# SwiGLUs: where the modulation chunks stand, and ScalarE's copies of running sums ahead of the late parts of a gate product

## The chip, the cores and the metric

One core of a Trainium2 chip runs one inference step. The metric is the device time of the program in microseconds; the median of three runs before the change is 2295.45 (2293.73 to 2296.03).

The core's engines work side by side, each through its own list of instructions in order, and wait for each other by semaphores: TensorE (PE, with its weight loads PEld), VectorE (DVE), ScalarE (ACT), GpSimd (POOL) and the queue that issues most loads (SP).

## The reference

Two layers of a hybrid diffusion model, on 128 prompt and 512 sample tokens of width 1024. Each layer has a SwiGLU, a mixer (convolution with a gMLP unit in the first layer, windowed attention in the second) and another SwiGLU, each with a modulated norm ahead of it and a gated residual behind:

```python
def swiglu(h, wg, wu, wd):
    return (jax.nn.silu(h @ wg) * (h @ wu)) @ wd

def modulation(cond, w_mod, b_mod):
    m = jax.nn.silu(cond) @ w_mod + b_mod
    return m.reshape(cond.shape[0], N_MOD, D_MODEL)
...
for l in range(DEPTH):
    mp = modulation(c_ctx[None, :], w_mod[l], b_mod[l])
    ms = modulation(c, w_mod[l], b_mod[l])
    xs = residual(xs, swiglu(pre(xs, ms, norm_w[l, 0], 0), *f1), ms, norm_w[l, 1], 0, 0.5)
    ...
    xs = residual(xs, swiglu(pre(xs, ms, norm_w[l, 4], 2), *f2), ms, norm_w[l, 5], 2, 0.5)
```

The inner width is 2816. All inputs are float32.

## The kernel before

**Numbers.** A float32 operand is split into a high part (ScalarE copies it, rounded) and a low part (VectorE subtracts the high part from the original). `mm3` multiplies with three matmuls: high by high, high by low, low by high. So each weight tile needs a load into one of three `raw` buffers (512 KB), a ScalarE copy and a VectorE subtraction before TensorE can use it, and the raw buffer is free again after the subtraction.

**A SwiGLU** (`ffn`) runs over 22 blocks `j` of 128 inner columns, cut into four parts: blocks 0 to 5, 5 to 10, 10 to 16 and 16 to 22 in the first SwiGLU (`PARTS`), 0 to 4, 4 to 10, 10 to 16 and 16 to 22 in the other three (`PARTS7`). Each part makes its gate products, then, but for the last part, a down-projection (`down`) multiplies them by their rows of `wd` and adds the result to `ys` in memory by GpSimd's DMA: ten products (two halves by five token tiles), each copied out of PSUM by ScalarE. The `between` list has what is issued after each of the ten; the `mods` list how many modulation chunks.

**Plain blocks.** The blocks of the first two parts of the first SwiGLU, and of the first part of the others, are computed as they stand (`unit`): for a group of 384 and one of 256 tokens, the gate and the up product of a block, then `glu`. `weights(j)` loads and splits a block's `wg` and `wu`. In the second part `sums_between(2)` puts one step of the running block sums (`block_sums`, 24 steps, mostly on VectorE) ahead of every second of a unit's eight `k` steps.

**Transformed blocks** (`group`). The later parts use a seven-product scheme on half-size operands. Per block `j` there are seven products `p1` to `p7` of 12 matmuls each; `p1`, `p6`, `p5` and `p3` accumulate one after another in the same PSUM tile `A[j]`, and the running sum is copied out between them (`e1`, `e6`, `e5`, ScalarE, into the tiles `sp` and `up`), before the next product may overwrite it. `p2` goes to another tile and `p7`, `p4` to a third, which VectorE adds or subtracts (`e2`, `e7`, `e4`). `e3` is the silu. `e4` ends with the product `s` of silu and up, a 128x640 tile, and its split into high and low: the gate product `gs[j]` that the down-projection reads. TensorE's order (`steps`) in the block of `j` is p1(j), p3(j-1), p6(j), p4(j-1), p7(j), p5(j), p2(j); p1, p2, p6, p7, p5 for a part's first block. `go` issues a product, then what copies out the products before it (`settle`), then the fill work of that step.

**Fill work.** `prep(j)` makes the weights of a block: g0 and g1 split the gate's raw tile (for p1 and p2), s2 forms sums of raw tiles on VectorE, t0 and t1 split those (p3, p6), s0 and s1 split another sum, `rawx`, which GpSimd's DMA accumulates (p7, p5), u0 and u1 split the rest (p4). The even ones run on ScalarE, the odd ones and s2 on VectorE. `fills(j+1)` spreads the next block's over the seven steps; the weights of a part's first block are made in the `between` list of the down-projection ahead of it.

**Modulation chunks.** The modulation of the coming sub-layers is computed on VectorE in the background: `background(n)` takes n chunks from a list; each (`mod_chunk`) loads 512 KB of `wmodT` into a raw buffer and reduces it twice against `cbc`, which `setup_cbc` loads and ScalarE runs through silu. 54 chunks are spread over the first SwiGLU, 33 each over the second and third, 8 over the fourth; `drain` does what is left at the end. `background_ahead` starts the load of the next chunk.

The order on TensorE, VectorE and ScalarE is that in which the code issues the instructions (`InOrder`, line 71, which is the line of all of them in the profile). SP's order is made by a scheduler, but it issues in order too: a load that waits for a raw buffer holds up those behind it.

Of the kernel before, what the change touches and what calls it, by code (L numbers as in the profile page):

```python
# [17 lines left out]
NT = 5  # L18
# [14 lines left out]
GA, GB = (0, 384), (384, 640)  # L33
GROUPS = [GA, GB]

PARTS7 = [(0, 4), (4, 10), (10, 16), (16, 22)]
HT = T // 2

# [51 lines left out]
class Builder:  # L90
# [550 lines left out]
    def ffn(self, l, i, h, lead, nxt, fetches, started=None):  # L641
# [4 lines left out]
        gs, ws = started or ({}, {})  # L646
        slot = 2 * i
        bounds = PARTS if started else PARTS7
        since = bounds[2][0] if started else bounds[1][0]

        def weights(j):
            if j not in ws:
                ws[j] = [self.take(*self.ffn_weight(l, i, j, w)) for w in ("wg", "wu")]
            return ws[j]

        def unit(j, g, inserts=None):
            if j not in gs:
                gs[j] = self.pair()
            self.glu(*self.proj2(weights(j), h, g, inserts), gs[j], g)
# [43 lines left out]
        def parts(pr):  # L703
            return [tuple(u[:, n * 512:n * 512 + 512] for u in pr) for n in range(pr[0].shape[-1] // 512)]
# [17 lines left out]
        def prep(j):  # L722


            def s2():
                r = raws["t", j] = raws["g", j]
                V.tensor_tensor(out=r[:, 512:1024], in0=raws["s", j][:, 512:1024], in1=r[:, 512:1024], op=ALU.add)
                V.tensor_tensor(out=r[:, 0:512], in0=r[:, 512:1024], in1=r[:, 0:512], op=ALU.add)

            g = halves("g", j, (2, j), (1, j))  # L730
            s = halves("s", j, (7, j), (5, j))
            t = halves("t", j, (3, j), (6, j))
            u = halves("u", j, (4, j), (4, j + 1)) if j in pairs else [lambda: None] * 2
            return dict(g0=g[0], g1=g[1], s2=s2, t0=t[0], t1=t[1], s0=s[0], s1=s[1], u0=u[0], u1=u[1])
# [61 lines left out]
        def e4(j):  # L796
            V.tensor_tensor(out=up[j][:, fh], in0=E.pop(j), in1=up[j][:, fh], op=ALU.subtract)
            s, u = sp.pop(j), up.pop(j)
            V.tensor_tensor(out=s, in0=s, in1=u, op=ALU.mult)
            gs[j] = self.pair()  # L800
            self.split(s, *gs[j])

        def run(fs):
            for f in fs:
                f()
# [13 lines left out]
        def sums_between(every=1):  # L819
            return {k: lambda: run([tops.pop(0) for _ in range(1) if tops]) for k in range(0, KC, every)}  # L820

        evacs = {p1: e1, p2: e2, p3: e3, p4: e4, p5: e5, p6: e6, p7: e7}
        late, done = [], set()

        def settle():

            for f, j in late[:]:
                if f is not p7 or (p5, j) in done:
                    late.remove((f, j))
                    evacs[f](j)  # L830
                    done.add((f, j))

        def go(f, j, *then):
            f(j)
            settle()
            late.append((f, j))
            run(then)

        def fills(n):

            if n >= NJ:
                return [[] for _ in range(7)]
            w = prep(n)
            return [[], [w["g0"]], [w["g1"]], [lambda: load_up(n), w["s2"]] if n in pairs else [w["s2"]], [w["t0"]],
                    [w["t1"], lambda: load_gate(n + 1) if n + 1 < ends[n] else None],
                    [w["s0"], w["s1"], lambda: load_sums(n + 2) if n + 2 < NJ else None]]

        def steps(j0, j1):

            r = [(p1, j0), (p2, j0), (p6, j0), (p7, j0), (p5, j0)]  # L850
            for j in range(j0 + 1, j1):
                r += [(p1, j), (p3, j - 1), (p6, j), (p4, j - 1), (p7, j), (p5, j), (p2, j)]
            return r

        def group(j0, j1, wd):


            fs = []
            ahead, mod = [self.background_ahead], [lambda: self.background(1)]
            for j in range(j0, j1):  # L860
                w = prep(j)
                f = fills(j + 1) if j + 1 < j1 else [[], [], wd[0:1], [], wd[1:2], [], wd[2:3]]
                u = [w["u0"], w["u1"]] if j in pairs else []
                if j == j0:
                    f = [u + ahead + f[1], f[2] + f[3], mod + f[4], f[5], ahead + f[6]]
                else:
                    f[0] = u + f[0]
                    if j + 1 < j1:
                        f[1] = f[1] + mod
                    if j + 2 < j1:  # L870
                        f[5] = f[5] + ahead
                fs += f
            for (p, j), f in zip(steps(j0, j1), fs):
                go(p, j, *f)
            go(p3, j1 - 1, *wd[3:4])
            go(p4, j1 - 1, *wd[4:])
            settle()

        ys = {(t, half): self.dram([P, 512], "ys") for t in range(NT) for half in range(2)}

        def down(j0, j1, pi, wd):

            gp = [gs.pop(j) for j in range(j0, j1)]
            loads, wd2 = wpieces(1, j0, j1)
            if j1 < since:
                between = [loads, [], [], [], [], [], [lambda: weights(j1)], [], [], []]
                mods = [0, 2, 2, 1, 1, 1, 0, 1, 1, 1]
            else:
                n = prep(j1)
                between = [loads, [], [], [lambda: load_gate(j1)], [],  # L890
                           [n["g0"], n["g1"]], [n["s2"], n["t0"]], [n["t1"], lambda: load_gate(j1 + 1)],
                           [lambda: load_up(j1), n["s0"]], [n["s1"], lambda: load_sums(j1 + 2)]]
                mods = [0, 2, 2, 1, 1, 0, 0, 0, 0, 0]
            n = j1 - j0 - 1
            for half in range(2):
                for t in range(NT):
                    if half or t > 1:
                        ps = self.ps()
                        self.proj_tok(ps, gp, (wd, wd2)[half], t)
                    elif t == 0:  # L900

                        two = self.ps(), self.ps()
                        for ks in (range(n), [n]):
                            for u in range(2):
                                self.proj_tok(two[u], gp, wd, u, ks)
                        ps = two[0]
                    else:
                        ps = two[1]
                    o = self.tmp(512)
                    copy(o, ps)  # L910
                    nc.gpsimd.dma_start(out=ys[t, half], in_=o, **(dict(accum_op=ALU.add) if pi else {}))  # L911
                    run(between.pop(0))
                    self.background(mods.pop(0))

        for pi, (j0, j1) in enumerate(bounds[:-1]):
            loads, wd = wpieces(0, j0, j1)
            if j0 >= since:
                group(j0, j1, loads)
            elif not started:
                load_sums(since)  # L920
                load_sums(since + 1)
                unit(1, GB, sums_between())
                weights(3)
                unit(2, GB, sums_between())
                todo = sums_between()
                todo[2] = lambda then=todo[2]: (then(), run(loads))
                unit(3, GA, todo)
                run(tops)
                unit(3, GB)
            else:  # L930
                if j0 == 0:
                    unit(1, GB)
                    self.setup_cbc()
                    unit(2, GA)
                    weights(3)
                    self.background(2)
                    unit(2, GB)
                    self.background(2)
                else:
                    load_sums(since)  # L940
                    load_sums(since + 1)
                for j in range(max(j0, 3), j1):
                    weights(j)
                    if j + 1 < j1:
                        weights(j + 1)
                    else:
                        run(loads)
                    for n, g in enumerate(GROUPS):
                        unit(j, g, sums_between(2) if j0 else None)
                        self.background(1 if j0 else 2)  # L950
                if j0:
                    run(tops)
            down(j0, j1, pi, wd)
        j0, j1 = bounds[-1]
        rows = self.gate_rows(l, slot, True)
# [1011 lines left out]
```

## Time and profile before

| | us |
|---|---|
| median of three runs | 2295.45 |
| profiled execution | 2296.32 |
| its span, first to last instruction | 2294.6 |
| TensorE busy | 2244.4 |
| VectorE busy | 1635.3 |
| ScalarE busy | 1042.9 |

The profile is of one execution. A row of the timeline begins with the time from the span's start and the length of the stretch, then engine, operation, what is written from what, the shape and how many instructions are merged in it; a bracket is the engine's idle time just before, and what ended it. A wait for several things is put down to the one that came last. Modulation chunks show as `scr<-raw,cbc`, weight splits as `w<-raw`, running-sum copies as ACT `tmp<-ps 128x320`, gate products' splits as `act<-tmp 128x640`. Matmuls `ps<-sum,w` occur only in transformed parts; their first ones start at 269 us in the first SwiGLU, at 802, 1249 and 1941 in the others.

### The profile page before, as it was taken

To read this page: it belongs to the slowest core of one execution; us is meant where nothing else is said; L and a number is where in the kernel's file an instruction comes from. 1 tells how busy PE (TensorE), PEld (TensorE's weight loads), DVE (VectorE), ACT (ScalarE), POOL (GpSimd) and SP (SyncE) were. 2 spreads that over 40 slices of the span, in tenths; PEclk is the share of its full clock that TensorE was granted. 3 is DMA by queue.
4 is the path that set the end of the run, shared out by engine and by line. 5 is a ranking of instruction groups with operands and counts; after the bars stand their busy time and mean duration, and the time that the engine had idled before them with its cause. 6 is when DMAs were issued, how large, how long until landed. Compare 5 with 4: busy or idle time off the path is not lost.

```text
span 2294.6 us, 35306 instructions
## 1 busy us (share of the span) xinstructions
PE 2244.4 (98%) x13692; PEld 2037.1 (89%) x13692; DVE 1635.3 (71%) x2738; ACT 1042.9 (45%) x1841; POOL 263.7 (11%) x364
## 2 busy tenths in 40 slices
PE   9989999999999999999999999999999999999998
PEld 7979898989889898989897989898976797989897
DVE  5688686876966885868778868687588578636366
ACT  5223343453246443434454434345568563434342
POOL 1000101011002011110021111101110021111100
PEclk9999999999999999999999999999999999999999
DMA  8574877553224477777546777765310345665645
GB/s 298 175 234 150 215 188 194 156 187 99 87 92 120 162 205 184 206 177 198 210 129 191 193 192 198 191 177 195 101 32 10 136 123 185 174 136 154 139 126 181
DMA packets 143049, 372.71 MB, mean 162 GB/s; under 512 B 15233, under 2 KB 21761, under 8 KB 142113
## 3 DMA queue, kind: packets, MB, share of 16 engines
q1 hardware_dynamic: 109328, 302.55, 38.9%
q0 software_dynamic: 33552, 67.90, 16.9%
q8 instruction: 107, 1.75, 0.3%
q14 instruction: 62, 0.50, 0.1%
HBM read 322.90 MB, written 42.25 MB: 159 GB/s over the span
## 4 chain that ended last, share of the span: by engine, by line
PE 69%; DVE 13%; DMA 7%; issue 5%; ACT 4%; POOL 1%; DVEq 0%; SPq 0%; ACTq 0%; POOLq 0%
PE ps L71 69%; DMA raw<-wmodT 4%; DVE scr L71 3%; DVE tmp L71 3%; DVE w L71 3%; DMA rawx<-ws 2%; ACT w L71 2%; ACT tmp L71 1%; DVE raw L71 1%; ACT act L71 1%; POOL nwq L71 1%; DVE Y L71 1%; DMA ys<-tmp 1%; DVE act L71 0%; ACT sum L71 0%
## 5 line engine op out<-in xcount | busy, mean ns | idle before, releaser
L71 PE MATMUL ps<-act,w 128*128 128x320 f32 (+6 forms) x6024 | 915.5, 319 | 21.3 <-DVE w L71 8.9
L71 PEld LDWEIGHTS ps<-act,w 128*128 128x128 f32 (+1 forms) x6024 | 847.5, 185 | 53.3 <-issue 18.3
L71 PE MATMUL ps<-w,act 128*128 128x512 f32 (+1 forms) x3480 | 781.6, 384 | 1.4 <-ACT act L71 1.3
L71 PEld LDWEIGHTS ps<-w,act 128*128 128x128 f32 x3480 | 624.3, 188 | 136.8 <-ACT act L71 2.6
L71 DVE TENSOR_TENSOR w<-raw,w 128x1024 fp32r<-128x1024 f32 (+1 forms) x340 | 409.1, 1216 | 205.1 <-ACT w L71 198.0
L71 PE MATMUL ps<-sum,w 128*128 128x320 f32 x3168 | 485.4, 311 | 13.8 <-ACT tmp L71 13.8
L71 PEld LDWEIGHTS ps<-sum,w 128*128 128x128 f32 x3168 | 473.6, 190 | 17.1 <-ACT tmp L71 17.0
L71 ACT ACTIVATE w<-raw 128x1024 fp32r<-128x1024 f32 (+1 forms) x340 | 350.6, 1047 | 205.6 <-DVE raw L71 107.3
L71 DVE CUSTOM_DVE_ANT_0 scr<-raw,cbc 128x1024 bf16<-128x1024 f32 x256 | 313.3, 1224 | 92.8 <-DMA raw<-wmodT 87.0
L71 ACT ACTIVATE tmp<-ps 128x320 f32<-128x320 f32 (+4 forms) x450 | 209.1, 469 | 371.8 <-PE ps L71 317.4
L71 ACT ACTIVATE act<-tmp 128x256 fp32r<-128x256 f32 (+4 forms) x238 | 114.9, 497 | 363.6 <-DVE tmp L71 363.5
L71 DVE TENSOR_TENSOR act<-tmp,act 128x256 fp32r<-128x256 f32 (+4 forms) x240 | 124.2, 525 | 117.0 <-ACT act L71 115.8
L911 POOL DMA_DIRECT2D ys<-tmp x120 | 90.9, 774 | 661.8 <-ACT tmp L71 653.5
L689 POOL DMA_DIRECT2D rawx<-ws x66 | 79.6, 1208 | 653.4 <-DMA rawx<-ws 189.3
L71 DVE TENSOR_TENSOR w<-rawx,w 128x1024 fp32r<-128x1024 f32 x66 | 80.8, 1224 | 27.3 <-ACT w L71 25.7
L71 DVE TENSOR_TENSOR tmp<-ps,tmp 128x320 f32<-128x320 f32 x132 | 64.0, 485 | 22.4 <-PE ps L71 21.3
L71 DVE TENSOR_TENSOR tmp<-tmp,tmp 128x640 f32<-128x640 f32 (+1 forms) x98 | 68.8, 715 | 6.4
L71 ACT ACTIVATE tmp<-ps,sh,G 128x256 f32<-128x256 f32 (+1 forms) x120 | 60.3, 525 | 22.8 <-PE ps L71 22.7
L71 ACT ACTIVATE w<-rawx 128x1024 fp32r<-128x1024 f32 x66 | 69.4, 1052 | 0.0
L71 DVE TENSOR_TENSOR tmp<-tmp,ps 128x320 f32<-128x320 f32 (+2 forms) x110 | 52.7, 479 | 18.0 <-ACT tmp L71 17.2
L71 ACT ACTIVATE tmp<-Y 128x1024 bf16<-128x1024 f32 (+1 forms) x35 | 32.6, 932 | 57.5 <-DVE Y L71 57.5
L71 ACT ACTIVATE Y<-X 128x1024 f32<-128x1024 f32 x30 | 31.7, 1058 | 54.6 <-DVE X L71 50.6
(162 smaller groups left out, 1242.0 us busy)
## 6 DMA issues: line engine op xcount, KB each, us to landing
raw<-wmodT SPq DMA_DIRECT2D x128, 512.0 KB, 4.7
raw<-ws SPq DMA_DIRECT2D x99, 512.0 KB, 4.6
raw<-wd SPq DMA_DIRECT2D x86, 512.0 KB, 4.0
rawx<-ws SPq DMA_DIRECT2D x66, 512.0 KB, 4.9
rawx<-ws POOLq DMA_DIRECT2D x66, 512.0 KB, 6.8
ys<-tmp POOLq DMA_DIRECT2D x120, 256.0 KB, 5.5
raw<-wg SPq DMA_DIRECT2D x22, 512.0 KB, 4.6
raw<-wu SPq DMA_DIRECT2D x22, 512.0 KB, 3.5
```

What stands on the lines that cost most here:

```text
L71: i = method(*args, **kw)
L689: nc.gpsimd.dma_start(out=r.rearrange("p (a b) -> p a b", a=2), in_=w[:, 1536:2048].unsqueeze(1).to_broadcast([P, 2, 512]), accum_op=ALU.add)
L911: nc.gpsimd.dma_start(out=ys[t, half], in_=o, **(dict(accum_op=ALU.add) if pi else {}))
```

## The change

It has four pieces. All instructions stay; only their places change.

1. The split of a gate product, until now the end of `e4`, is kept in a list (`pend`) and issued at the next `p3`, after that step's running-sum copies.
2. In `group`, u0 and u1 move from a block's first step to its second, the chunk from the second to the fifth (in a part's first block from the third to the fourth, the others' fills with it one step along).
3. In `down`, the number of chunks goes by the part's length: four behind a part of four blocks, six behind five, seven behind six, where it was six behind all. In the first SwiGLU's first down-projection `weights(j1)` is issued one product sooner, behind six chunks of that list in place of seven.
4. In the first SwiGLU `setup_cbc` is issued one unit sooner, four chunks follow at once, and the units of the first two parts have the numbers of `MODS1`; the sums are put on every third step.

```diff
+MODS1 = {(3, 0): 2, (3, 1): 1, (4, 0): 1, (4, 1): 1, (5, 0): 1, (5, 1): 0, (6, 0): 1, (6, 1): 0, (7, 0): 1, (7, 1): 0,
+         (8, 0): 1, (8, 1): 0, (9, 0): 2, (9, 1): 2}
...
             V.tensor_tensor(out=s, in0=s, in1=u, op=ALU.mult)
-            gs[j] = self.pair()
-            self.split(s, *gs[j])
+
+            def parts():
+                gs[j] = self.pair()
+                self.split(s, *gs[j])
+
+            pend.append(parts)
...
             late.append((f, j))
+            if f is p3:
+
+                flush()
             run(then)
+
+        def flush():
+            while pend:
+                pend.pop(0)()
...
                 if j == j0:
-                    f = [u + ahead + f[1], f[2] + f[3], mod + f[4], f[5], ahead + f[6]]
+                    f = [ahead, u + f[1], f[2] + f[3], f[4] + mod, f[5] + ahead + f[6]]
                 else:
-                    f[0] = u + f[0]
+                    f[1] = u + f[1]
                     if j + 1 < j1:
-                        f[1] = f[1] + mod
+                        f[4] = f[4] + mod
...
             settle()
+            flush()
...
             if j1 < since:
-                between = [loads, [], [], [], [], [], [lambda: weights(j1)], [], [], []]
-                mods = [0, 2, 2, 1, 1, 1, 0, 1, 1, 1]
+                between = [loads, [], [], [], [], [lambda: weights(j1)], [], [], [], []]
+                mods = [0, 2, 2, 2, 0, 0, 1, 1, 1, 1]
...
-                mods = [0, 2, 2, 1, 1, 0, 0, 0, 0, 0]
+
+                mods = {4: [0, 1, 1, 1, 1], 5: [0, 2, 2, 1, 1], 6: [0, 2, 2, 2, 1]}[j1 - j0]
+                mods += [0] * (2 * NT - len(mods))
...
                 if j0 == 0:
+                    self.setup_cbc()
                     unit(1, GB)
-                    self.setup_cbc()
+                    self.background(4)
                     unit(2, GA)
...
-                        unit(j, g, sums_between(2) if j0 else None)
-                        self.background(1 if j0 else 2)
+                        unit(j, g, sums_between(3) if j0 else None)
+                        self.background(MODS1[j, n])
```

What it does to three rows of instructions, as the programs have them (the changed one's lines are three further on, so 71 is 74):

On ScalarE, at the start of the second SwiGLU's first transformed part (block 4): `rawx` is s0, the `128x512` row the last copy of the down-projection, the `w<-raw` rows u0 of block 4 and g0 of block 5, `tmp<-ps 128x320` the copy e1. Before:

```order
L71 ACTIVATE tmp_7944<-ps_7931 128x512
L71 ACTIVATE tmp_7963<-ps_7950 128x512
L71 ACTIVATE w_7968<-rawx_7437 128x1024
L71 ACTIVATE tmp_7984<-ps_7971 128x512
L71 ACTIVATE w_8004<-raw_7966 128x1024
L71 ACTIVATE w_8010<-raw_7948 128x1024
L71 ACTIVATE tmp_8026<-ps_7991 128x320
L71 ACTIVATE w_8049<-raw_7948 128x1024
```

and now:

```order
L74 ACTIVATE tmp_7932<-ps_7919 128x512
L74 ACTIVATE tmp_7951<-ps_7938 128x512
L74 ACTIVATE w_7956<-rawx_7437 128x1024
L74 ACTIVATE tmp_7972<-ps_7959 128x512
L74 ACTIVATE tmp_8007<-ps_7979 128x320
L74 ACTIVATE w_8010<-raw_7954 128x1024
L74 ACTIVATE w_8014<-raw_7936 128x1024
L74 ACTIVATE tmp_8008<-ps_7979 128x320
```

The copy e1 has moved ahead of u0 and g0. The second running-sum copy (e6) moves ahead of t0 of block 5 with it.

On ScalarE, one block on in the same part: `act<-tmp 128x640` is the high part of a gate product, the `tmp<-ps` rows the copies of running sums. Before, the gate product's split of block 4 stands ahead of t0, e5, s0, u0 and the next e1:

```order
L71 ACTIVATE tmp_8026<-tmp_8026 128x320
L71 ACTIVATE tmp_8118<-ps_8090 128x320
L71 ACTIVATE act_8174<-tmp_8026 128x640
L71 ACTIVATE w_8178<-raw_8067 128x1024
L71 ACTIVATE tmp_8118<-ps_8090 128x320
L71 ACTIVATE w_8212<-rawx_7988 128x1024
L71 ACTIVATE w_8234<-raw_8155 128x1024
L71 ACTIVATE tmp_8250<-ps_8219 128x320
```

and now:

```order
L74 ACTIVATE tmp_8007<-tmp_8007 128x320
L74 ACTIVATE tmp_8106<-ps_8078 128x320
L74 ACTIVATE w_8158<-raw_8067 128x1024
L74 ACTIVATE tmp_8106<-ps_8078 128x320
L74 ACTIVATE w_8196<-rawx_7976 128x1024
L74 ACTIVATE tmp_8230<-ps_8203 128x320
L74 ACTIVATE act_8233<-tmp_8007 128x640
L74 ACTIVATE w_8237<-raw_8139 128x1024
```

The split has moved behind the copies e5 (`tmp_8106`) and e1 of the next block (`tmp_8230`), and stands ahead of u0 and g0.

On VectorE, in the second SwiGLU's first down-projection: `scr` rows are halves of chunks, `w<-raw` here g1 of block 4, the `raw` rows s2. The short reads of the sums between the `scr` rows are left out. Before, the second half of the fourth chunk, the fifth, the sixth, g1 and s2:

```order
L71 ISA scr_7842,mraw_105<-raw_7838,cbc 128x1024
L71 ISA scr_7864,mraw_105<-raw_7862,cbc 128x1024
L71 ISA scr_7866,mraw_105<-raw_7862,cbc 128x1024
L71 ISA scr_7886,mraw_105<-raw_7884,cbc 128x1024
L71 ISA scr_7888,mraw_105<-raw_7884,cbc 128x1024
L71 TENSOR_TENSOR w_7907<-raw_7860,w_7906 128x1024
L71 TENSOR_TENSOR raw_7860<-rawx_7437,raw_7860 128x512
L71 TENSOR_TENSOR raw_7860<-raw_7860 128x512
```

and now the third chunk, the fourth and last, g1 and s2:

```order
L74 ISA scr_7852,mraw_105<-raw_7850,cbc 128x1024
L74 ISA scr_7854,mraw_105<-raw_7850,cbc 128x1024
L74 ISA scr_7874,mraw_105<-raw_7872,cbc 128x1024
L74 ISA scr_7876,mraw_105<-raw_7872,cbc 128x1024
L74 TENSOR_TENSOR w_7895<-raw_7848,w_7894 128x1024
L74 TENSOR_TENSOR raw_7848<-rawx_7437,raw_7848 128x512
L74 TENSOR_TENSOR raw_7848<-raw_7848 128x512
```

Two chunks less stand ahead of g1 and s2 there.

More of the change, by code (lines that the diff above doesn't have):

```diff
@@ L822, in ffn @@
         evacs = {p1: e1, p2: e2, p3: e3, p4: e4, p5: e5, p6: e6, p7: e7}
-        late, done = [], set()
+        late, done, pend = [], set(), []
         def settle():
```

## The prediction

> **What bounds the kernel now.** First the page's table of engines: does anything but TensorE set the time?
>
> ```profile
> span 2294.6 us, 35306 instructions
> PE 2244.4 (98%) x13692; PEld 2037.1 (89%) x13692; DVE 1635.3 (71%) x2738; ACT 1042.9 (45%) x1841; POOL 263.7 (11%) x364
> ```
>
> TensorE is idle 50 us in all. No matmul is removed, so the most the change can win is that idle time, and what a slower clock costs behind it. Next the matmuls in order of time, cut to the rows with a gap: the first figure is the start, the second the row's length, the bracket the idle time ahead of it and what ended it. Of the first four gaps only the first and last row are shown (6.19 us in all), as for the next four (2.90).
>
> ```profile
> 146.68 1.01 PE L71 MATMUL ps<-act,w 128*128 128x384 f32 x2 [4.98 <-ACT w L71]
> 150.59 43.67 PE L71 MATMUL ps<-act,w 128*128 128x384 f32 x285 [0.25 <-DVE w L71]
> 195.08 0.79 PE L71 MATMUL ps<-act,w 128*128 128x384 f32 x3 [0.82 <-DVE w L71]
> 212.59 13.51 PE L71 MATMUL ps<-act,w 128*128 128x384 f32 x91 [0.35 <-DVE w L71]
> 261.98 3.50 PE L71 MATMUL ps<-act,w 128*128 128x320 f32 x22 [0.77 <-DVE w L71]
> 269.14 7.09 PE L71 MATMUL ps<-sum,w 128*128 128x320 f32 x36 [3.66 <-ACT tmp L71]
> 291.86 2.01 PE L71 MATMUL ps<-act,w 128*128 128x320 f32 x12 [1.57 <-ACT tmp L71]
> 795.14 5.02 PE L71 MATMUL ps<-act,w 128*128 128x320 f32 x22 [1.76 <-DVE w L71]
> 802.30 7.10 PE L71 MATMUL ps<-sum,w 128*128 128x320 f32 x36 [2.14 <-ACT tmp L71]
> 1070.07 2.01 PE L71 MATMUL ps<-act,w 128*128 128x320 f32 x12 [2.08 <-ACT tmp L71]
> 1241.98 3.47 PE L71 MATMUL ps<-act,w 128*128 128x320 f32 x22 [1.48 <-DVE w L71]
> 1249.14 7.09 PE L71 MATMUL ps<-sum,w 128*128 128x320 f32 x36 [3.69 <-ACT tmp L71]
> 1399.26 2.02 PE L71 MATMUL ps<-act,w 128*128 128x320 f32 x12 [0.93 <-ACT tmp L71]
> 1934.18 3.49 PE L71 MATMUL ps<-act,w 128*128 128x320 f32 x22 [1.10 <-DVE w L71]
> 1941.35 7.09 PE L71 MATMUL ps<-sum,w 128*128 128x320 f32 x36 [3.68 <-ACT tmp L71]
> ```
>
> All of these lie in the four SwiGLUs, at places the change touches: 33.3 us, with five smaller gaps at the late products (0.2 to 0.4 us, 1.3 together). The waits on 2.1 us and more are by "ACT tmp", a copy of a running sum out of PSUM, or by "w", the split of a weight.
>
> Each long gap costs more than itself. 36 matmuls take 7.09 us behind it, but 5.66 where none precedes; the table of windows (length, PE, PEld, DVE, ACT and POOL busy, granted clock, DMA share, GB/s) shows why:
>
> ```profile
> 919.43 5.66 PE L71 MATMUL ps<-sum,w 128*128 128x320 f32 x36
> ...
> 150.00:154.00 4.00, 3.75 (x13) 3.41 (x12) 3.58 (x6) 0.74 (x2) 1.60 (x3) 0.50 0.95 302
> 795.00:799.00 4.00, 3.86 (x17) 3.86 (x18) 2.69 (x4) 2.43 (x4) 0.59 (x2) 0.62 0.38 131
> ```
>
> Behind a gap the granted clock falls to about half for some microseconds: 1.43 us lost behind each 3.7 us gap and behind 802.30; 1.55 at 795.14 (22 matmuls take 5.02, against 3.47 at 1241.98). It happened behind 1.76 and 2.14 us, not behind 2.08 (2.01 us for 12 at 1070.07, as at 291.86).
>
> [...]
>
> **The change, part by part.** A modulation chunk is two vector instructions of 1.22 us and two short reads, 2.53 us, and a 512 KB load:
>
> ```profile
> L71 DVE CUSTOM_DVE_ANT_0 scr<-raw,cbc 128x1024 bf16<-128x1024 f32 x256 | 313.3, 1224 | 92.8 <-DMA raw<-wmodT 87.0
> ...
> raw<-wmodT SPq DMA_DIRECT2D x128, 512.0 KB, 4.7
> ```
>
> No work is added: 54, 33, 33 and 8 chunks before and after. They only move.
>
> *Second to fourth SwiGLU, first down-projection (four chunks in place of six).*
>
> ```profile
> 791.45 1.23 DVE L71 CUSTOM_DVE_ANT_0 scr<-raw,cbc 128x1024 bf16<-128x1024 f32 x1 [1.35 <-DMA raw<-wmodT]
> 793.87 1.22 DVE L71 TENSOR_TENSOR w<-raw,w 128x1024 fp32r<-128x1024 f32 x1
> 799.91 2.01 ACT L71 ACTIVATE w<-raw 128x1024 fp32r<-128x1024 f32 x2
> 801.81 0.44 ACT L71 ACTIVATE tmp<-ps 128x320 f32<-128x320 f32 x1
> ```
>
> The split g1 (793.87) stands behind the sixth chunk; without the fifth and sixth it can start near 787 (the fourth chunk's load, now issued behind the gate's, allowed for with 4.7 us), 6 us ahead of TensorE's arrival at 793, and s2, t and s move up behind it. The first e1 (801.81) also loses the 2.01 us of two weight copies ahead of it. Both gaps go: 3.90, 5.17 and 4.78 us, with clock 2.98, 1.43 and 1.43. **-6.9, -6.6, -6.2.** What is late next is s: s1 ends near 794, and p7 wants it three products of 1.8 us behind 793, so some 4 us of cover; with that gone the gap would come back there by what is missing. Bounds: nothing, and these sums.
>
> *Copies ahead of late parts.*
>
> ```profile
> 289.80 0.74 ACT L71 ACTIVATE act<-tmp 128x640 fp32r<-128x640 f32 x1 [7.78 <-DVE tmp L71]
> 291.39 0.42 ACT L71 ACTIVATE tmp<-ps 128x320 f32<-128x320 f32 x1
> ```
>
> ScalarE stood 7.78 us at the split of a gate product, because VectorE was held ahead of it; e5 stood behind, and p3 behind e5. Now e5 goes first, and the chunk stands behind e4. All eight such gaps (1.57, 2.08, 0.93 and the five small ones) go: **-5.9**; from 0 to -5.9. The deferred split is queued ahead of u0 and g0, and only the down-projection reads it, a block or more later, so its own cost is hidden.
>
> *Six-long parts (five of them): a seventh chunk.*
>
> ```profile
> 905.74 0.33 SPq L695 DMA_DIRECT2D raw<-ws  x1
> 908.16 1.22 DVE L71 TENSOR_TENSOR w<-raw,w 128x1024 fp32r<-128x1024 f32 x1
> 915.94 3.65 PE L71 MATMUL ps<-act,w 128*128 128x320 f32 x24
> 918.58 0.42 ACT L71 ACTIVATE tmp<-ps 128x320 f32<-128x320 f32 x1
> ```
>
> The seventh load takes the raw buffer free at 905.74, lands 4.7 us later, near 910.4, and its chunk ends at 913.0, so g1 slips 4.8 us. g1 ends at 909.4 now and TensorE comes at 915.9; of that cover 1.7 us are left. But behind it g1, s2, t0, two copies of the down-projection, s0, a third copy and e1 take about 6.5 us from the chunk's end, by their lengths in this stretch: e1 ends near 919.5, where now it ends at 919.0 even with the two weight copies ahead of it. So 0 to 1 us each, 2 us more where the load is slow: **+3** for five, bounds 0 and +20 (3 us of wait and 1 us of clock each).
>
> *First SwiGLU, up to the weights of j = 5.*
>
> ```profile
> 73.14 0.55 DVE L71 TENSOR_TENSOR tmp<-tmp,ps 128x384 f32<-128x384 f32 x1 [7.06 <-ACT tmp L71]
> 77.51 1.22 DVE L71 CUSTOM_DVE_ANT_0 scr<-raw,cbc 128x1024 bf16<-128x1024 f32 x1
> 78.47 0.38 ACT L71 ACTIVATE tmp<-ps 128x256 f32<-128x256 f32 x1 [2.33 <-PE ps L71]
> ```
>
> 19 chunks precede these weights in both (12 and 7; 13 and 6), but the first starts at 66 in place of 77.5, in a stretch where VectorE idles. Four chunks fill 66 to 76, and the loads of j = 3 queue behind them on SP: their splits end near 81, an estimate from 4.7 us a load, where TensorE is done with j = 2 at 78.4 (what ScalarE waited for at 78.47): some 2.4 us of new wait there and at j = 4. From then on raw buffers pace the chain; followed load by load, the last split of j = 5 ends near 146.6, not 150.5. **-4.0**, whatever TensorE waited earlier; bounds -6.2 and +2.4. Without the long gap the half clock from 150 to 154 goes, half of 3.4 us: **-1.7**.
>
> *Second part (8 chunks for 10, sums on every third step).*
>
> ```profile
> L71 DVE TENSOR_TENSOR tmp<-tmp,tmp 128x640 f32<-128x640 f32 (+1 forms) x98 | 68.8, 715 | 6.4
> ```
>
> At the weights of j = 8 VectorE has one chunk and four sum steps (0.7 us or more each, as this row) less ahead of them, 5 us against waits of 1.2; at j = 9 two chunks and six steps. The gaps of 2.90 go, but the weights of j = 6 now have four chunks ahead in place of three: **-2.5**, bounds -2.9 and +1.
>
> *Its down-projection keeps six chunks*, with two more just ahead. Of 4.43 us the two weight copies (2.0) go, and g1's 0.77: 1.5 stay; the clock may fall or not. **-3.6**, bounds 0 and -5.9.
>
> Sum: -6.9 -6.6 -6.2 -5.9 +3 -5.7 -2.5 -3.6 = **-34.4 us**. The profiled execution took 2296.3 us (1.7 around its span), so 2261.9; it lies 0.9 above the median of the runs shown, so about 2262 for a median.
>
> **The rivals.**
> - *The first part is not relieved.* The chunks only move the queue: TensorE loses 2.4 us at j = 3 and 4, and the wait at j = 5 stays. For it: 19 chunks in both, and SP issues in order. Against: the 7.06 us of idle VectorE time are used. -34.4 +5.7 +2.4: 2270.
> - *The seventh chunk is late.* The loads ahead of it in such a stretch waited for DMA, as at 791.45. At 4 us for each of five: +17 more, 2279.
> - *The waits are only handed on*, to the next operand each time: within 4.6 us of 2295.
> - *Slower: the deferred split binds every block.* The copy e6 writes the buffer that the deferred split still reads, and p5 overwrites PSUM behind e6. A window of one block, with the columns as above:
>
> ```profile
> 837.29:849.57 12.28, 12.28 (x86) 12.28 (x85) 11.10 (x17) 5.57 (x9) 1.20 (x1) 1.00 0.74 201
> ```
>
> VectorE is busy for 11.10 of 12.28 us. By the new order the split's end comes near 3.8 us into a block and p5 near 8.8, so 4 us of slack. If VectorE runs later than that, TensorE waits in each of some 55 blocks; from 0.65 us each the gain is gone, at 1 us it is 20 us slower: 2316.
>
> **How the numbers follow.** Forecast 2262 (2253 to 2268): 0.57. First part not relieved, about 2270: 0.17. Late seventh chunk, alone or with it, to 2285: 0.14. Handed on: 0.07. Slower: 0.05. The most that can go is 33.3 us of gaps and 9.0 of clock, 42: 2253, the low end; 2280 leaves out the last two and the worst of the third. Faster by over 0.2% (4.6 us, about what a measurement can tell from no change): 0.88; same 0.07; slower 0.05.
>
> **What would show it.** Right: no gaps near the starts of the first transformed parts in the second to fourth SwiGLU, and granted clock 1.00 there; no p3 behind "ACT tmp"; the wait at j = 5 under 3 us. Wrong: gaps at the fourth or fifth SwiGLU part boundary behind a seven-chunk down-projection; new gaps at j = 3; small gaps in each block ended by "ACT tmp". What makes the whole wrong is VectorE as the bound in the blocks.

## The result and the profile after

| | before | after |
|---|---|---|
| median, us | 2295.74 (2293.73 to 2297.75) | 2271.28 (2269.04 to 2276.8) |
| profiled execution, us | 2296.32 | 2272.71 |
| its span, us | 2294.6 | 2270.9 |

The ratio is 0.9891 (95% interval 0.9875 to 0.9907): 24.5 us faster, of 34.4 forecast. The page of the changed kernel, its first lines, and the waits of TensorE (waited in all, times, the longest):

```profile
span 2270.9 us, 35340 instructions
PE 2231.6 (98%) x13692; PEld 2027.2 (89%) x13692; DVE 1624.8 (72%) x2738; ACT 1042.5 (46%) x1841; POOL 264.2 (12%) x364
...
PE ps L74 <- ACT tmp L74: 13.8, 16, 2.6
PE ps L74 <- DVE w L74: 9.3, 10, 1.6
```

TensorE is busy 12.8 us less for the same matmuls, since hardly any of them run at half clock now (its mean granted clock is 0.999, before 0.993), and idle for 39.3 us, not 50.2. The long waits are gone, but 16 waits on copies of running sums (13.8 us) are left. The timeline of TensorE in the changed kernel shows which:

```profile
141.57 18.61 PE L74 MATMUL ps<-act,w 128*128 128x384 f32 x121
...
779.71 3.65 PE L74 MATMUL ps<-act,w 128*128 128x320 f32 x24
783.20 5.44 PE L74 MATMUL ps<-sum,w 128*128 128x320 f32 x36
...
920.72 2.01 PE L74 MATMUL ps<-act,w 128*128 128x320 f32 x12 [2.57 <-ACT tmp L74]
924.60 7.08 PE L74 MATMUL ps<-sum,w 128*128 128x320 f32 x46 [1.58 <-DVE w L74]
...
1369.29 5.33 PE L74 MATMUL ps<-sum,w 128*128 128x320 f32 x34 [1.14 <-DVE w L74]
...
1485.88 2.01 PE L74 MATMUL ps<-act,w 128*128 128x320 f32 x12 [1.31 <-ACT tmp L74]
1489.35 7.09 PE L74 MATMUL ps<-sum,w 128*128 128x320 f32 x46 [1.17 <-DVE w L74]
```

The unit of j = 5 (141.57) and the first transformed part of the second SwiGLU (779.71, 783.20) begin without a gap. The rows from 920 on are new: they lie in parts behind a seven-chunk down-projection, where first the p3 of the second block waits for e5 and then the p6 of the third block for t1. To see what each place is worth, the next table takes, for each stretch, its length in the profiled execution after less that before; the lengths are differences of the start times of the matmul rows at its two ends.

| stretch | forecast | measured |
|---|---|---|
| first SwiGLU, first two parts | -8.2 | -13.9 |
| its first transformed part (10 to 16) | -5.4 | -2.4 |
| first transformed part of the second, third, fourth | -19.7 | -20.9 |
| **five parts behind seven chunks** | -1.1 | **+14.5** |
| all else | 0 | -1.0 |
| span | -34.4 | -23.7 |

(The forecast of the second row is -3.6 for the down-projection and -1.78 for the two gaps at late products that it held, 1.57 and 0.21; that of the fourth is +3 less the other such gaps, 4.1.) The five lose 3.1, 3.9, 2.8, 1.5 and 3.2 us. Most of their waits are of these two kinds: 6.2 us at the p3 of a second block and 6.2 us at the p6 of a third. In the first blocks TensorE waits 2.9 us for e1 and e6. One of the five is the second SwiGLU's blocks 10 to 16, which start at 895.19 here. Its rows of VectorE, ScalarE, SP (`SPq`) and GpSimd in the timeline of the changed kernel:

```profile
888.01 1.23 DVE L74 CUSTOM_DVE_ANT_0 scr<-raw,cbc 128x1024 bf16<-128x1024 f32 x1 [1.64 <-DMA raw<-wmodT]
...
896.15 1.23 DVE L74 TENSOR_TENSOR w<-rawx,w 128x1024 fp32r<-128x1024 f32 x1 [0.69 <-ACT w L74]
897.40 0.33 SPq L691 DMA_DIRECT2D rawx<-ws  x1
905.57 1.21 POOL L692 DMA_DIRECT2D rawx<-ws  x1 [7.81 <-DVE mraw L74]
917.84 0.69 DVE L74 TENSOR_TENSOR raw<-rawx,raw 128x512 f32<-128x512 f32 x1 [8.80 <-issue]
919.28 1.06 ACT L74 ACTIVATE w<-raw 128x1024 fp32r<-128x1024 f32 x1 [9.39 <-DVE raw L74]
920.25 0.42 ACT L74 ACTIVATE tmp<-ps 128x320 f32<-128x320 f32 x1
920.50 1.22 DVE L74 CUSTOM_DVE_ANT_0 scr<-raw,cbc 128x1024 bf16<-128x1024 f32 x1
923.33 1.22 DVE L74 TENSOR_TENSOR w<-raw,w 128x1024 fp32r<-128x1024 f32 x1
```

Read it downwards. The seventh chunk (888.01) stands ahead of everything, 2.5 us long and 1.64 late by its load. s1 (896.15) is the last reader of a `rawx` buffer; only then does SP load the sums of block 12 into it (897.40), 2.2 us behind the part's start. GpSimd adds to them (905.57), and VectorE's s2 can begin when that has landed, at 917.84, after 8.80 us without work. t0 (919.28) needs s2, e5 (920.25) stands behind t0 on ScalarE, and p3 waits for e5. Then VectorE does the block's modulation chunk (920.50) before t1 (923.33), and p6 waits for t1.

### The profile page after: what moved, and what is told of

It is laid out like the page before. It is cut to its first block, busy times and chain, and to the rows that moved or that the text cites. A ratio compares the mean times of both kernels' runs of the same rounds, so it can differ in the third digit from the quotient of the medians.

```text
span 2270.9 us, 35340 instructions
## 1 busy us (share of the span) xinstructions
PE 2231.6 (98%) x13692; PEld 2027.2 (89%) x13692; DVE 1624.8 (72%) x2738; ACT 1042.5 (46%) x1841; POOL 264.2 (12%) x364
## 4 chain that ended last, share of the span: by engine, by line
PE 78%; DVE 9%; DMA 5%; issue 3%; ACT 3%; POOL 1%; SPq 0%; DVEq 0%; ACTq 0%; POOLq 0%
PE ps L74 78%; DMA rawx<-ws 3%; DVE tmp L74 3%; DVE scr L74 2%; DVE w L74 2%; ACT w L74 1%; DMA raw<-wmodT 1%; DVE raw L74 1%; POOL nwq L74 1%; DVE Y L74 1%; ACT act L74 1%; ACT tmp L74 1%; ACT sum L74 0%; DMA raw<-ws 0%; DMA X<-x 0%
## 5 line engine op out<-in xcount | busy, mean ns | idle before, releaser
L74 PEld LDWEIGHTS ps<-sum,w 128*128 128x128 f32 x3168 | 467.7, 188 | 19.5 <-ACT tmp L74 10.2
L74 DVE TENSOR_TENSOR raw<-rawx,raw 128x512 f32<-128x512 f32 x66 | 45.7, 692 | 50.8 <-DMA rawx<-ws 34.7
L74 ACT ACTIVATE tmp<-ps,sh,G 128x256 f32<-128x256 f32 (+1 forms) x120 | 60.5, 527 | 22.7 <-PE ps L74 22.6
```

Source lines behind the costliest of these rows:

```text
L74: i = method(*args, **kw)
```

## The experiments

Three theories of the lost 14.5 us. **A**: the seventh chunk delays s1, and with it the chain above. **B**: the chunk's new place in the block, between s2 and t1, makes p6 late. **C**: the deferred split of the gate product costs. Two theories of the 13.9 us won at the start: **F1**, the early chunks in VectorE's idle time; **F2**, the sooner weights. Stretches are from each run's profiled execution against that of before; each ratio is to the kernel before, run beside it.

| kernel | median, us | ratio to before (95%) | first two parts | 10 to 16 | three | five |
|---|---|---|---|---|---|---|
| changed | 2271.28 | 0.9891 (0.9875 to 0.9907) | -13.9 | -2.4 | -20.9 | +14.5 |
| changed, again | 2275.08 | 0.9899 (0.9880 to 0.9917) | -13.5 | +0.7 | -21.8 | +14.3 |
| six chunks | 2260.12 | 0.9855 (0.9835 to 0.9876) | -13.5 | -0.1 | -21.1 | -0.6 |
| old step | 2271.13 | 0.9896 (0.9877 to 0.9915) | -12.3 | -1.7 | -19.2 | +6.7 |
| six, old step | 2255.66 | 0.9840 (0.9821 to 0.9859) | -13.4 | -2.9 | -19.5 | -6.0 |
| deferral and steps alone | 2284.87 | 0.9962 (0.9947 to 0.9976) | -0.2 | -3.6 | -1.8 | -6.6 |
| seventh chunk last | 2266.71 | 0.9874 (0.9855 to 0.9892) | -12.5 | +0.2 | -21.8 | +4.8 |
| weights not sooner | 2274.82 | 0.9899 (0.9873 to 0.9926) | -11.8 | -0.6 | -13.3 | +12.6 |
| early chunks late | 2282.03 | 0.9945 (0.9930 to 0.9959) | -2.2 | -0.5 | -19.9 | +11.4 |
| chunk counts alone | 2293.83 | 0.9982 (0.9969 to 0.9994) | +0.9 | -1.2 | -14.3 | +15.2 |

How far the stretches scatter can be read off where four of these kernels have the same code: the five parts stand at +14.5, +14.3, +12.6 and +11.4, so a difference of 3 us there says little.

**Six chunks.** The edit; the chunk left over goes to the last block of a part:

```diff
-mods = {4: [0, 1, 1, 1, 1], 5: [0, 2, 2, 1, 1], 6: [0, 2, 2, 2, 1]}[j1 - j0]
+mods = {4: [0, 1, 1, 1, 1], 5: [0, 2, 2, 1, 1], 6: [0, 2, 2, 1, 1]}[j1 - j0]
...
                     if j + 1 < j1:
                         f[4] = f[4] + mod
-                    if j + 2 < j1:
+                    else:
+                        f[1] = f[1] + mod
+                    if j + 1 < j1:
                         f[5] = f[5] + ahead
```

> The changed kernel with six chunks in place of seven in the down-projections behind parts of six blocks; the chunk that is left over goes to the second step of the last block of each transformed part, where VectorE has no weights of a next block to make. Theory A (the seventh chunk holds up s1, with it the load of the next sums into the same buffer, and the whole chain of s2, t0 and e5 behind it): the five parts behind those down-projections, which lose 14.5 us between them against before, lose nothing or win up to 4; 2271 - 14 to 18 = 2253 to 2257, and no gap over 1 us at the second block's p3. Theory B (the chunk's new place in the block, between s2 and t1, makes p6 late): the gaps of 1.15 to 1.58 us ahead of the x46 or x34 rows stay, five of them, 6 us; 2261 to 2265. Theory C (the deferred split of the gate product is what costs): no gain, 2271.

The five come to -0.6 us, as A had it; the median is 3 us above A's figure, with 2256.56 for the fastest run. One of the five, in the first SwiGLU, still loses 2.6 us: s2 is late there too (VectorE stands 7.40 us ahead of it), and the same p3 and p6 wait 1.14 and 1.15 us. The same four steps in the timeline of this kernel, whose part starts at 897.36:

```profile
895.01 1.23 DVE L74 TENSOR_TENSOR w<-rawx,w 128x1024 fp32r<-128x1024 f32 x1 [0.85 <-ACT w L74]
896.26 0.33 SPq L691 DMA_DIRECT2D rawx<-ws  x1
903.07 1.21 POOL L692 DMA_DIRECT2D rawx<-ws  x1 [3.71 <-DMA rawx<-ws]
911.25 0.69 DVE L74 TENSOR_TENSOR raw<-rawx,raw 128x512 f32<-128x512 f32 x1
```

The load is issued 1.1 us ahead of the part's start, not 2.2 behind it, and s2 comes 13.9 us after that start in place of 22.7. Of the 8.8 us between the two, 3.3 are the later issue, which is the chunk's; the rest is made by the loads. From issue to landing, the first line of each pair (stretch 897 to 918 of the changed kernel, 896 to 912 of this one) is SP's, the second GpSimd's:

```profile
rawx<-ws SPq DMA_DIRECT2D x2, 512.0 KB, 9.2
rawx<-ws POOLq DMA_DIRECT2D x1, 512.0 KB, 12.2
...
rawx<-ws SPq DMA_DIRECT2D x2, 512.0 KB, 5.8
rawx<-ws POOLq DMA_DIRECT2D x1, 512.0 KB, 6.9
```

Later by 3 us, the same accumulation takes 12.2 us in place of 6.9. It runs together with other loads: SP issued a chunk's at 905.26, one of block weights at 906.39 and the next sums' at 907.53. That it is these loads was not tried by itself.

**The chunk at its old step**, with seven chunks:

```diff
-f = [ahead, u + f[1], f[2] + f[3], f[4] + mod, f[5] + ahead + f[6]]
+f = [ahead, u + f[1], f[2] + f[3], mod + f[4], f[5] + ahead + f[6]]
...
                     if j + 1 < j1:
-                        f[4] = f[4] + mod
+                        f[1] = f[1] + mod
```

> The changed kernel with the chunk of each block back at the step where it stood before, ahead of g1 and s2 in place of behind s2; seven chunks as in the change. Theory A: the five parts still lose some 14 us, since what is late there is late before the block begins; 2268 to 2272. Theory B: the five gaps ended by the split t1 (6 us) go, and VectorE's idle time ahead of the late s2 takes the chunk instead; 2263 to 2266. Theory C: 2271.

The five come to +6.7 us in this execution: half of the loss is gone, so A alone does not hold; B's 6 us are there (7.8, against a scatter of 3). The rows agree: in the changed kernel the third block's p6 waits for t1 in all five parts, 6.2 us together, and here in none. The median did not show it (2271.13, runs from 2265.41 to 2273.32; the ratio is that of the changed kernel), so B rests on the stretches and rows.

**Both edits.**

> Both edits: six chunks behind six blocks, and the chunk of each block at its old step. Theory A alone: as with six chunks alone, 2253 to 2257. A and B together, each for its own part: 2253 to 2256, some 6 us under the kernel with six chunks alone. Theory C: 2271.

2255.66 us, and -6.0 in the five, 5.4 under six chunks alone: in the stretches the two causes add up within the scatter. The ratios of the two kernels with six chunks overlap, so by time alone they are not told apart.

**The deferral and the steps alone**, on the kernel before (`pend`, `flush` and `fills` in `group`; the rest as before).

> The kernel before with the deferred split of the gate product and the new steps of u0, u1 and the chunk alone; six chunks behind every part, first SwiGLU as before. By the prediction the eight gaps ahead of p3 go, 5.9 us, and e1 ahead of u0 and g0 takes some 2 us from each of the long gaps in front of the first transformed parts: 2282 to 2290. Theory A: the five parts win 4 us between them, no loss there. Theory B: gaps of 1.2 us ended by t1 appear in these parts here too, 6 us, so 2288 to 2296. Theory C: the five parts lose 10 us or more against before here as well: 2300.

The five win 6.6 us and the first transformed part 3.6; C falls. So does B as a cost by itself: the chunk stands at its new step here too, and nothing is lost in the five. A p6 does wait for t1, 1.14 us each time, in the first transformed parts of the first and second SwiGLU (at 290.42 and 819.44), and in both s2 is late: VectorE had stood 6.80 and 6.14 us ahead of it for the load of the sums. So far as these runs show, the new step costs only where s2 is already late. The first transformed parts of the other three win just 1.8 by e1 ahead of u0 and g0, where 6 was expected.

**The chunk counts alone**, on the kernel before:

```diff
-mods = [0, 2, 2, 1, 1, 0, 0, 0, 0, 0]
+mods = {4: [0, 1, 1, 1, 1], 5: [0, 2, 2, 1, 1], 6: [0, 2, 2, 2, 1]}[j1 - j0]
+mods += [0] * (2 * NT - len(mods))
```

> The kernel before with the numbers of chunks in the down-projections alone (four, six or seven by the part's length); splits, steps and the first two parts as before. If the four chunks carry the gain at the first transformed parts of the second to fourth SwiGLU: 19 to 21 us won there, as in the change. If the copy e1 ahead of u0 and g0 is needed for it too: 8 to 14. Theory A (seventh chunk): the five parts behind seven chunks lose 12 to 16 us against before here too, with the chunk at its old step; in all 2286 to 2292. Theory B (place in the block alone): those parts lose 0 to 3, 2274 to 2278.

The five lose 15.2 us with the chunk at its old step and the split in its old place, so the seventh chunk is enough for the loss; the path through s1 is what the rows above add. Not all of it is that path here: 6.8 us are waits of the second block's p3 for e5, and 6.0 us waits of the first block's p6 for e1, which still stands behind two weight copies. At the first transformed parts of the other three SwiGLUs the four chunks win 14.3 us by themselves and e1 ahead of the weight copies 1.8 (the kernel above); together they win 20.9. The timeline of this kernel, again at blocks 10 to 16 of the second SwiGLU:

```profile
940.48 2.01 PE L71 MATMUL ps<-act,w 128*128 128x320 f32 x12 [2.31 <-ACT tmp L71]
```

It is the wait of 920.72 above, at the same product.

**The seventh chunk last**, behind s1:

```diff
-mods = {4: [0, 1, 1, 1, 1], 5: [0, 2, 2, 1, 1], 6: [0, 2, 2, 2, 1]}[j1 - j0]
-mods += [0] * (2 * NT - len(mods))
+mods = {4: [0, 1, 1, 1, 1], 5: [0, 2, 2, 1, 1], 6: [0, 2, 2, 1, 1]}[j1 - j0]
+mods += [0] * (2 * NT - len(mods) - 1) + [j1 - j0 == 6]
```

> The changed kernel with the same seven chunks, but the seventh behind the last step of the down-projection (behind s1), not ahead of the weights of the next part's first block. Theory A1 (the seventh chunk costs because s1 comes later, with it the load into the sums' buffer and GpSimd's accumulation, which then shares the DMA engines with the next chunk's load and took 12.2 us in place of 6.9): the five parts come out as with six chunks, about -0.6 us against before in place of +14.5; 2256 to 2261. Theory A2 (VectorE's time and the three raw buffers do not hold a seventh chunk in that stretch wherever it stands): 2267 to 2272.

The five come to +4.8 us: 9.7 of 14.5 go though VectorE has as much to do. The chain is sooner, in the same rows of this kernel's timeline, whose part starts at 896.58:

```profile
895.48 0.33 SPq L691 DMA_DIRECT2D rawx<-ws  x1
901.44 1.21 POOL L692 DMA_DIRECT2D rawx<-ws  x1 [2.87 <-DVE w L74]
911.10 0.69 DVE L74 TENSOR_TENSOR raw<-rawx,raw 128x512 f32<-128x512 f32 x1
```

The load is issued 1.1 us ahead of the part's start, as with six chunks, and this part takes as long as there, 1.0 us less than before. The 5.4 us that separate the five from six chunks speak for A2, the chunk's own time and buffer in that stretch; they are not much above the scatter. They lie mostly in two other parts, where a p3 waits 2.08 and 2.07 us for its e5 and its 12 matmuls take 2.79 and 3.44 us (at 1025.16 and 1350.22), against 2.01 at 920.72 in the changed kernel. The time, 2266.71, lies between both theories.

**The first SwiGLU.** Two kernels undo one piece each of the changed one. Weights as before:

```diff
-between = [loads, [], [], [], [], [lambda: weights(j1)], [], [], [], []]
-mods = [0, 2, 2, 2, 0, 0, 1, 1, 1, 1]
+between = [loads, [], [], [], [], [], [lambda: weights(j1)], [], [], []]
+mods = [0, 2, 2, 1, 1, 1, 0, 1, 1, 1]
```

> The changed kernel with the first SwiGLU's first down-projection as before: the weights of j = 5 issued behind seven chunks and one product later. Theory F1 (the early chunks in VectorE's idle time carry the 13.9 us of the first two parts): up to 2.5 us of wait come back at j = 5, the half clock stays away; 2271 to 2274. Theory F2 (the sooner weights carry it): 4 us or more of wait and the half clock behind it come back, 7 to 9 us; 2278 to 2280.

Four chunks back from unit 2 to j = 3 and 4:

```diff
+unit(1, GB)
 self.setup_cbc()
-unit(1, GB)
-self.background(4)
 unit(2, GA)
...
-MODS1 = {(3, 0): 2, (3, 1): 1, (4, 0): 1, (4, 1): 1,
+MODS1 = {(3, 0): 2, (3, 1): 2, (4, 0): 2, (4, 1): 3,
```

> The changed kernel with the load of cbc one unit later, as before, and the four early chunks given to the units of j = 3 and j = 4 instead; as many chunks as in the change ahead of the weights of j = 5, weights sooner. Theory F1: the wait at j = 5 and the half clock come back, 5 to 10 us in the first two parts; 2276 to 2281. Theory F2: no more than 1 us; 2270 to 2272.

TensorE's rows around the weights of j = 5, of the first of these kernels and, below the dots, of the second:

```profile
144.44 5.86 PE L74 MATMUL ps<-act,w 128*128 128x384 f32 x32 [0.58 <-DVE w L74]
...
148.12 1.01 PE L74 MATMUL ps<-act,w 128*128 128x384 f32 x2 [4.69 <-ACT w L74]
149.38 0.69 PE L74 MATMUL ps<-act,w 128*128 128x384 f32 x1 [0.25 <-DVE w L74]
150.52 1.01 PE L74 MATMUL ps<-act,w 128*128 128x384 f32 x2 [0.45 <-ACT w L74]
```

Without the sooner weights there is 0.58 us of gap; with the chunks late the 4.69 us come back, with the half clock (0.53 mean granted clock from 146 to 157). F1 holds: the early chunks are worth 11.7 us of the 13.9, more than the 10 it had at most, and the sooner weights 2.1, within the scatter. (The stretches without the sooner weights are from the slowest of its four runs, 2282.32.) What they use, from 66 to 78 us, by the table of windows, of before and then of after (DVE is the third busy time):

```profile
66.00:78.00 12.00, 12.00 (x85) 12.00 (x84) 3.96 (x6) 4.34 (x5) 0.00 (x0) 1.00 0.16 29
...
66.00:78.00 12.00, 11.70 (x82) 11.39 (x82) 10.81 (x18) 3.18 (x5) 0.00 (x0) 1.00 0.57 179
```

VectorE had 8.0 us of 12 free there; now it has 1.2.

**Fewer chunks still.** On the kernel with both edits: five behind parts of five and six blocks, two in a part's last block:

```diff
-mods = {4: [0, 1, 1, 1, 1], 5: [0, 2, 2, 1, 1], 6: [0, 2, 2, 1, 1]}[j1 - j0]
+mods = {4: [0, 1, 1, 1, 1], 5: [0, 1, 2, 1, 1], 6: [0, 1, 2, 1, 1]}[j1 - j0]
...
+                    if j + 1 == j1:
+                        f[1], f[3] = f[1] + ahead, f[3] + mod
```

> The kernel with six chunks and the old step of the chunk, with one chunk less again in the down-projections behind parts of five and six blocks (five), and two in the last block of each transformed part. If what is left in the first parts behind them (2.2 us of gap at 250 us with 0.8 of the first SwiGLU, small ones elsewhere) is still the chunks ahead of g1 and s1: 3 to 5 us under that kernel, 2250 to 2253. If those gaps are due to loads alone: 2255, as there; if a second chunk in the last block is late: 2257 or more.

A miss: 2277.16 us, ratio 0.9930 (0.9907 to 0.9952). Five parts now have a wait of 2.2 to 5.5 us at the p4 of their last block. Two of these rows of TensorE, and below the dots one row of ScalarE and one of VectorE ahead of the first:

```profile
858.96 3.56 PE L74 MATMUL ps<-sum,w 128*128 128x320 f32 x12 [4.94 <-DVE tmp L74]
...
1307.92 3.57 PE L74 MATMUL ps<-sum,w 128*128 128x320 f32 x12 [5.52 <-DVE tmp L74]
...
856.19 1.06 ACT L74 ACTIVATE w<-raw 128x1024 fp32r<-128x1024 f32 x1 [4.79 <-DMA raw<-wd]
857.28 1.22 DVE L74 TENSOR_TENSOR w<-raw,w 128x1024 fp32r<-128x1024 f32 x1 [4.95 <-ACT w L74]
```

The 12 matmuls wait for VectorE's e7 and take 3.56 us, where 12 behind the gap at 920.72 in the changed kernel take 2.01 at a granted clock of 1.00. But VectorE's time is not what is short. Both chunks are done at 849.7, and VectorE later stands 4.95 us: e7 is behind the low part of a `wd` weight (857.28), that is behind ScalarE's copy (856.19), and the copy waited 4.79 us for the weight's load. In the five parts this copy waits 2.3 to 5.6 us. So a load is late, not the chunk; that the second chunk's raw buffer delays it was not tried by itself. One chunk in that block costs little (the kernels with six).

**Five chunks behind five blocks only**, else six and the old step; and both kernels again beside it, on one chip:

> The kernel with six chunks behind six blocks and the old step, now with five behind the first SwiGLU's part of five blocks; the one left over fits in the last block of the last transformed part. If the gap of 2.2 us there, ended by the split of a weight, and the half clock behind it come from the chunks ahead of that split: 3 to 5 us less, 2250 to 2253. If not: 2255.

> Six chunks and the old step again, in more rounds: 2254 to 2257, ratio to before 0.982 to 0.985.

> The changed kernel again, on the same chip as these: 2269 to 2274, some 15 us above the kernel with six chunks and the old step.

2255.81 us, 0.9812 (0.9793 to 0.9831), for five; 2257.57, 0.9821 (0.9802 to 0.9840), for six with the old step; 2275.08 for the changed kernel. The two are not told apart. Rows at the first SwiGLU's first transformed part, of six with the old step (its earlier execution) and then of five:

```profile
250.02 5.02 PE L74 MATMUL ps<-act,w 128*128 128x320 f32 x22 [2.22 <-DVE w L74]
255.30 3.79 PE L74 MATMUL ps<-sum,w 128*128 128x320 f32 x24 [0.26 <-ACT tmp L74]
...
248.19 3.49 PE L74 MATMUL ps<-act,w 128*128 128x320 f32 x22 [0.67 <-DVE w L74]
253.46 7.08 PE L74 MATMUL ps<-sum,w 128*128 128x320 f32 x36 [1.78 <-ACT tmp L74]
```

A chunk less moves most of the wait from the split g1 to e1, and the slow matmuls with it: 22 behind g1 take 3.49 us in place of 5.02, but 36 behind e1 take 7.08 (5.44 at 783.20 in the changed kernel, at a granted clock of 1.00). What remains there is still open. Six chunks with the old step is a version that beats both kernels, by 17.5 us on the changed one on this chip.

## Why the prediction was half right

The sign and the widest range held (2271 in 2253 to 2280), but not the 2253 to 2268 given to the forecast itself. By its number 2271 is the rival of a first part that is not relieved (2270), which did not happen: that part won more than forecast. That the range held is in part luck, since two errors partly cancel: the five parts came out 15.6 us worse, the first two parts 5.7 us better.

1. **First down-projection of the second to fourth SwiGLU: right** (-19.7; -20.9). Four chunks alone make 14.3 of it, and the other pieces on top of them the rest.
2. **"Six-long parts: a seventh chunk, +3" is the step that failed.** It followed the delay of g1 down ScalarE's row to e1, found 0 to 1 us, and stopped. The same delay passes through s1, which frees the buffer for the sums of the block after next; that load, GpSimd's accumulation, s2, t0 and e5 stand behind it, and they are not on the row that was counted. That row held its size: the first blocks' waits at e1 and e6 come to 2.9 us in the five. The other path made most of the rest, 6.2 us at the second blocks' p3 and 6.2 at the third blocks' p6. With the chunk counts alone the five lose 15.2 us, inside the bound of +20 that was given. The rival of a late seventh chunk had the place and about the price (4 us for each), but its reason, a chunk's load that lands late, is 1.64 us of the chain shown (at 888.01), not the 8.8.
3. **Copies ahead of late parts, "all eight go": right alone, not in company.** On the kernel before, with the new steps, the deferral won 10.2 us in the six parts that hold these gaps, more than the 5.9. In the change the e5 that no longer stood behind a split stood behind t0, because s2 was late. The sentence that the chunk stands behind e4 counted that as a gain; where s2 is late, it stands in t1's way (7.8 us with seven chunks). The deferral itself won beside seven chunks too: 15.2 us are lost with the chunk counts alone, 6.7 with the old step of the chunk, the deferral and the new step of u0 and u1.
4. **First SwiGLU, first two parts: mechanism right, size too small** (-8.2; -13.9). The new waits at j = 3 and 4, taken as 2.4 us, measured 0.30, 0.34 and 0.19, and the wait at j = 5 vanished instead of falling to 1. The half clock was priced from 150 to 154 us; it lay over 7.5 us of the unit's work:

```profile
146.68:154.22 7.54, 6.33 (x16) 4.92 (x17) 6.13 (x9) 2.51 (x4) 1.60 (x3) 0.50 0.82 274
```

   Half of the 6.33 us of TensorE's work at a granted clock of 0.50 is 3.2 us, not 1.7. The 6.2 us of the first four gaps, the next 2.9 and 3.2 make 12.3 of the 13.9; the rest was not traced.
5. **The first transformed part behind them: -5.4 forecast, -2.4 measured** in one execution, +0.7 in another of the same kernel. Of the 4.43 us of gaps at its start 3.67 are left, where 1.5 were forecast (1.66 by its own terms): g1 waits longer than before, 1.11 us for 0.77, still behind the last chunk of its down-projection, and e1 (1.79) and e6 (0.77) come late after it. At the third block's p6 a new wait of 1.15 us stands (278.21), by the late s2 again, without a seventh chunk. Over the whole of the other execution the mean granted clock is 0.996, not 0.999. The deferral alone wins 3.6 there.
6. **The slower rival did not come.** No part shows a p5 that waits block by block: apart from first blocks p5 waits for e6 twice, 0.90 us at 1050.64 and 0.38 at 1375.00. In the part with the row at 924.60 nothing over 0.3 us follows until the next part.

## What to carry over

When work is added ahead of a producer, follow every buffer that the delayed instructions free, not only the row of the engine that comes next: here a buffer freed 3 us later cost a load, an accumulation that ran among other loads, and two engines' queues. Undoing the parts of a change one by one found a version that is better than the whole: it leaves out the seventh chunk, which lost 15 us with or without the other pieces, and the chunk's new step, which by the stretches cost only where s2 was late. Background work belongs where the engine's idle time is measured (8.0 us of 12 at 66 us): moving it there was worth 11.7 us, issuing the weights behind it sooner 2.1.

## What the runs showed of the hardware

In these runs the half clock does not follow from the length of a gap. TensorE's gap of 2.57 us at 920.72 in the changed kernel left the 12 matmuls behind it at 2.01 us. In the kernel whose weights were not sooner, the first row below has a shorter gap at a product that its edit does not touch, and the window shows the clock behind it; the kernel with the seventh chunk last has the third row:

```profile
814.57 3.24 PE L74 MATMUL ps<-sum,w 128*128 128x320 f32 x12 [1.98 <-ACT tmp L74]
815.00:818.00 3.00, 3.00 (x13) 3.00 (x13) 2.86 (x5) 1.21 (x2) 1.20 (x1) 0.50 0.14 24
...
1025.16 2.79 PE L74 MATMUL ps<-act,w 128*128 128x320 f32 x12 [2.08 <-ACT tmp L74]
```

The table gives the matmuls of the row behind each gap and, where a window shows it, the mean granted clock over the row (from 815 to 818 us in the sixth):

| kernel | gap, us | ends at | matmuls behind it | granted clock |
|---|---|---|---|---|
| before | 1.76 | 795.14 | 22 in 5.02 us | 0.66 |
| before | 2.14 | 802.30 | 36 in 7.10 us | 0.76 |
| before | 2.08 | 1070.07 | 12 in 2.01 us | 1.00 |
| before | 1.48 | 1241.98 | 22 in 3.47 us | 1.00 |
| changed | 2.57 | 920.72 | 12 in 2.01 us | 1.00 |
| weights not sooner | 1.98 | 814.57 | 12 in 3.24 us | 0.50 |
| seventh chunk last | 2.08 | 1025.16 | 12 in 2.79 us | - |

The longest of these gaps has full clock behind it and the gap of 1.76 us has not; gaps of 2.08 us have 12 matmuls in 2.01 us behind them in one kernel and in 2.79 in another. What decides was not shown: no run moved a gap on purpose.

Such slow matmuls are part of why single executions scatter. With the same code there, the three first transformed parts came to -13.3 us in the kernel without the sooner weights, not -20.9: two of them had a gap of 1.98 and 1.79 us each (at 814.57 and 1954.21) that the changed kernel did not show, and the 12 matmuls behind it took 3.24 and 2.90 us, where 12 of this kind take 2.03 at 258.27 in the changed kernel.
